# A two-layer hybrid decoder step on one core: ScalarE work behind VectorE issued later, branches in another order, pooling spread out, gates one pair ahead

## The chip, the core and the metric

The kernel runs on one core of one Trainium2 chip. The metric is device time in microseconds (us) of the whole launch, here the median of three runs. The engines named below are TensorE (PE in the profile), VectorE (DVE), ScalarE (ACT), GpSimd (POOL) and SyncE (SP, which here only issues transfers). Each works through its own instructions in order.

## The reference, cut to what matters

One step of two equal layers over 544 columns (512 prompt tokens and 8 x 4 new ones), all in f32 with a model width of 1024. A layer is a feed-forward block, a mixer, a second feed-forward block and a gated per-layer embedding. The change lies in the mixer alone:

```
h = rmsnorm(x, g_mix);  z = h @ w_in
u_a, v_a, b_gate, c_gate, x_b, x_c, gates = split(z)
v_a = layernorm(gelu(v_a));  y_a = (gelu(u_a) * (tril(w_s) @ v_a + b_s)) @ a_out      # branch a
y_b = (b_gate * short_conv(c_gate * x_b)) @ b_out                                      # branch b
y_c = ((window_mean(x_c, 2|4|8|16) - x_c) @ c_w * c_scale) @ c_out                     # branch c
g = sigmoid(gates)
x = x + (g0*y_a + g1*y_b + g2*y_c) @ w_o
```

The short convolution has three taps; the pooling has four channel groups with windows of 2, 4, 8 and 16 positions.

## The kernel before, in words

Activations lie transposed: 8 tiles of 128 channels x 544 columns. Every f32 product is made of three products of split operands, a high part rounded on ScalarE (L245 for weights, L362 for activations) and a low part, the difference, on VectorE (L250, L367). Weights come in units of 128 x 512 through the SP queue (L224, L227, L231), some with an accumulating transfer of the POOL queue on top (L232). `unit()` (L260) prepares them ahead of their use: the low part four units ahead, the high part five, the sum (L238) six, the load fifteen.

Two output tiles of `w_in` are made together by `pair()` (L736), which calls `s_pair()` (L568): a Strassen-Winograd scheme of seven half-size products, W21, R2, R3, W22, R1, W12, R4, each 12 matmuls (L326), 84 in all. Products that add into the same accumulator X need X copied by ScalarE first (L582 after W21, before R3; L584 after R3, before R1; L589 after R1, before R4). VectorE reads the others (L585, L587, L590, L592). The accumulators lie in four PSUM tiles of two halves each, taken in turn. Products of the branches' own output weights and of `w_o` go through `gemm()` (L306, matmuls of L303).

The order of the work is the order of the code. Each engine's queue is in that order, and what is to be issued later is put on two lists: `later` (a function and the number of ticks until it is issued) and `bg`, a queue of functions that `background()` spreads over a number of ticks. `tick()` (L175) runs once for each weight unit: once per product of `s_pair`, and once per `gemm` of four blocks. `flush()` issues at once all that is left.

The mixer runs: the first convolution pair by `gemm`; the v rows (L833, 120 matmuls of 512 columns into five PSUM halves; ScalarE takes the gelu of each, L807, VectorE its mean and variance, L808 and L809); three convolution pairs, each followed by `conv_in` (L746: product with the gate on VectorE, L751; two copies and the first tap on ScalarE, L756 to L765; two further taps on VectorE, L767); two pairs for `b_gate`; branch b; the pairs of x_c with the pooling steps (`pool_in` L898 to L910 on ScalarE, window sums L926, means L934, small fix-ups L939 and L940, then the split L362 and L367); a pair of u; branch c with `c_mix` (four small products by `c_w`, scaled by L961); the other pair of u; the four spatial products (`spatial`, L997); branch a; the product by `w_o`. In a branch, each step makes a pair of gates (sigmoid by L738 to L741) and then two `gemm`s, whose results are multiplied by the gates (L876) and added up (L881). `merge` (L856) splits the sum for `w_o`.

Of the kernel before, what the change touches and what calls it, by code (L numbers as in the profile page):

```python
# [17 lines left out]
KD = D // P  # L18
# [20 lines left out]
LOADS = 9  # L39
USE_MERGE = 51  # L40
AHEAD = 4
# [62 lines left out]
class Kern:  # L104
# [252 lines left out]

    def split_later(self, t_, aps, sls, n=1):
        nc = self.nc
        a, b = self.rpair()  # L360
        hi, lo, src = a[0][:, :], b[0][:, :], t_[0][:, :]
        nc.scalar.activation(hi, src, AF.Copy)  # L362
        aps.append((hi, lo))
        sls.extend((a, b))

        def fin():
            nc.vector.tensor_sub(lo, src, hi.bitcast(F32))  # L367
            self.drop(t_)

        if n:  # L370
            self.later.append((n, fin))
        return fin

# [350 lines left out]
    def mix(self, l, inp, nxt):  # L724
# [11 lines left out]
        def pair(z1, z2, f=None):  # L736
            s1, s2 = self.slot(), self.slot()
            self.s_pair("w_in", l, z1, z2, sets, s1, s2, (lambda out, ps: nc.scalar.activation(out, ps, f)) if f else None)  # L738
            if f:
                nc.scalar.activation(s2[0][:, :HT], s2[0][:, :HT], f)  # L740
                nc.scalar.activation(s1[0][:, :], s1[0][:, :], f)  # L741
            return s1, s2
# [3 lines left out]
        def conv_in(j, c_, x_, z_=None):  # L746
            c, x = c_[0], x_[0]
            sv = self.nt(self.cst[:, :], CB + TS)
            xp, xs_ = (z_[0][:, :SEQ], self.nt(z_[0][:, SEQ:T], TS)) if z_ else (x[:, CB:CCOLS], sv[:, :, CB:])
            nc.vector.memset(x[:, :CB], 0.0)  # L750
            nc.vector.tensor_mul(x[:, CB:CCOLS], xp, c[:, :SEQ])  # L751
            nc.vector.tensor_mul(sv[:, :, CB:], xs_, self.nt(c[:, SEQ:T], TS))
            if z_:
                self.drop(z_)
            o = j * NS * CB
            nc.scalar.activation(self.cso[:, SO_CP + j * CB:SO_CP + (j + 1) * CB], x[:, CCOLS - CB:CCOLS], AF.Copy)  # L756
            o = SO_CS + j * NS * CB
            nc.scalar.activation(self.nt(self.cso[:, o:o + NS * CB], CB), sv[:, :, TS:], AF.Copy)
            ys = self.nt(c[:, SEQ:T], TS)
            for k in range(3):  # L760
                o = PB_CW + (l * 3 + k) * G + j
                wk = self.par[:, o:o + 1]
                if k == 0:
                    nc.scalar.activation(c[:, :SEQ], x[:, 0:SEQ], AF.Copy, scale=wk)
                    nc.scalar.activation(ys, sv[:, :, 0:TS], AF.Copy, scale=wk)  # L765
                else:
                    nc.vector.scalar_tensor_tensor(c[:, :SEQ], x[:, k:k + SEQ], wk, c[:, :SEQ], op0=ALU.mult, op1=ALU.add)  # L767
                    nc.vector.scalar_tensor_tensor(ys, sv[:, :, k:k + TS], wk, ys, op0=ALU.mult, op1=ALU.add)
            self.drop(x_)
            conv[j] = c_  # L770

        def conv_state(j):
# [94 lines left out]

        def branch(br, ys, wn, mid=None):
            for m in range(0, KD, 2):
                ts = pair(Z_G + br * KD + m, Z_G + br * KD + m + 1, AF.Sigmoid)  # L870
                if m == 0 and mid:
                    mid()
                for i, t_ in enumerate(ts):
                    t = t_[0]
                    py, = self.gemm([(wn, l, m + i, ys, 0)])
                    nc.vector.tensor_mul(self.v2(t[:, :]), self.pv(py), self.v2(t[:, :]))  # L876
                    if len(macc) < KD:
                        macc.append(t_)
                        continue
                    mc = macc[m + i][0]  # L880
                    nc.vector.tensor_add(mc[:, :], mc[:, :], t[:, :])  # L881
                    self.drop(t_)
                    if br == 0 and self.used < USE_MERGE and len(merged) == m + i:
                        merge(m + i)
# [5 lines left out]
        self.background([v_stat] + [lambda i=i, f=f: f(i) for i in range(5) for f in (v_norm, v_bias)], 30)  # L890
        self.extra = EXTRA[4]
        branch(1, yb, "b_out", conv_done)
        self.drop(*yb_s)
        pooled, pooled_s = {}, {}
# [17 lines left out]
        def pool_steps(j, z_):  # L912
# [30 lines left out]

            return [begin] + [double] * (win.bit_length() - 1) + [mean, lambda: pool_out(j, st)]

# [29 lines left out]
        self.flush()  # L975
# [6 lines left out]
        u_in(0)  # L982

        def c_mid():
            self.flush()
            c_mix()

        branch(2, yc, "c_out", c_mid)
        self.drop(*yc_s)

        ya, ya_s = [], []

        def spatial(g):
# [13 lines left out]
            self.drop(us[g])  # L1007
            self.split_later(t_, ya, ya_s)
            if g == G - 1:
# [287 lines left out]
```

## Time and profile before

| | |
|---|---|
| median of 3 runs | 2452.64 us (2451.56 to 2452.81) |
| the profiled execution | 2452.78 us, its span 2451.1 us, granted clock 0.995 |
| busy, PE / DVE / ACT / POOL | 98% / 76% / 50% / 9% of the span |
| chain that ended last | PE 93%, DVE 3%, ACT 3%, issue 1% |
| mean DMA rate | 135 GB/s |

The page gives each engine's busy share; the chain that ended last follows the run back from its end and says at each step which engine held it up. The two mixers lie at about 389 to 799 us and 1598 to 2008 us of the span. A matmul that runs right behind another shows as one run with it; a gap in a timeline has in brackets how long the engine waited, and for whom.

### The profile page before, as it was taken

Reading aid. Unit: us, or ns where it says so; the run is one execution under the profiler, and the core shown is the slowest. Engines: PE = TensorE matmul, PEld = TensorE weight load, DVE = VectorE, ACT = ScalarE, POOL = GpSimd, SP = SyncE. Lnnn points to the kernel's source line nnn. Section 1 sums busy time; section 2 is a strip of 40 time slices with the busy share of each in tenths; the row PEclk is TensorE's granted clock in tenths of the full one; section 3 lists DMA queues with packets and bytes.
Section 4 is the critical chain, followed back from the end, with each engine's and each line's share of the span. In section 5 each row is a group of like instructions: output and inputs, shape, how many; then the busy total and the mean of one; then the engine's idle time right before and its main releaser. Section 6 shows DMA issues by size and latency. Waiting matters only on the chain.

```text
span 2451.1 us, 48091 instructions
## 1 busy us (share of the span) xinstructions
PE 2407.8 (98%) x18848; PEld 2386.7 (97%) x18848; DVE 1861.8 (76%) x3439; ACT 1215.0 (50%) x2357; POOL 226.3 (9%) x276
## 2 busy tenths in 40 slices
PE   8999999998999999999999999999989999999997
PEld 8999998998999999999999999989989999999997
DVE  7776777878678777768777776778787778777675
ACT  6444444646446544445554444546455554544452
POOL 1101000111110110100010110001101001101000
PEclk9999999999999999999999999999999999999999
DMA  6555561665554555555255554526545536556521
GB/s 204 141 146 143 147 168 27 175 146 130 151 148 121 134 143 144 154 133 161 59 144 136 144 156 127 162 60 159 149 126 146 151 95 154 153 125 158 139 84 37
DMA packets 180034, 329.78 MB, mean 135 GB/s; under 512 B 20256, under 2 KB 22560, under 8 KB 179808
## 3 DMA queue, kind: packets, MB, share of 16 engines
q1 hardware_dynamic: 141264, 255.92, 33.8%
q0 software_dynamic: 36672, 68.51, 16.7%
q8 instruction: 148, 2.42, 0.4%
q10 hardware_dynamic: 1872, 2.29, 0.3%
q14 instruction: 78, 0.64, 0.1%
HBM read 323.64 MB, written 2.99 MB: 133 GB/s over the span
## 4 chain that ended last, share of the span: by engine, by line
PE 93%; DVE 3%; ACT 3%; issue 1%; DMA 0%; DVEq 0%; ACTq 0%
PE ps L326 49%; PE ps L303 38%; PE ps L1094 2%; PE ps L833 2%; ACT s L245 1%; PE ps L531 0%; PE ps L517 0%; DVE s L926 0%; DVE s L250 0%; DVE s L1006 0%; ACT s L807 0%; ACT s L362 0%; DVE s L483 0%; ACT L738 0%; DVE s L238 0%
## 5 line engine op out<-in xcount | busy, mean ns | idle before, releaser
L326 PE MATMUL ps<-s,s 128*128 128x272 f32 x10332 | 1321.2, 289 | 18.2 <-ACT s L582 14.6
L326 PEld LDWEIGHTS ps<-s,s 128*128 128x128 f32 x10332 | 1307.7, 189 | 24.1 <-ACT s L582 18.4
L303 PE MATMUL ps<-s,s 128*128 128x272 f32 x7536 | 965.1, 288 | 8.2 <-ACT s L444 7.0
L303 PEld LDWEIGHTS ps<-s,s 128*128 128x128 f32 x7536 | 953.0, 189 | 9.8 <-ACT s L444 6.9
L250 DVE TENSOR_TENSOR s<-s,s 128x512 fp32r<-128x512 f32 x1211 | 812.5, 686 | 21.8 <-ACT s L245 19.9
L245 ACT ACTIVATE s<-s 128x512 fp32r<-128x512 f32 x1211 | 702.6, 623 | 230.8 <-DVE s L238 225.8
L232 POOL DMA_DIRECT2D s<-in_wts x246 | 210.7, 875 | 1941.4 <-DMA s<-in_wts 761.7
L582 ACT ACTIVATE s<-ps 128x272 f32<-128x272 f32 x123 | 48.7, 396 | 468.9 <-PE ps L326 468.9
L665 DVE SCALAR_TENSOR_TENSOR x<-ps,x 128x544 f32<-128x544 f32 x128 | 92.7, 724 | 184.1 <-PE ps L303 182.3
L238 DVE TENSOR_TENSOR s<-s,s 128x512 f32<-128x512 f32 x246 | 168.7, 686 | 0.0
L585 DVE TENSOR_TENSOR s<-ps,s 128x272 f32<-128x272 f32 x123 | 54.3, 442 | 113.8 <-ACT s L584 112.3
L584 ACT ACTIVATE s<-ps 128x272 f32<-128x272 f32 x123 | 48.8, 397 | 103.6 <-PE ps L326 102.2
L590 DVE TENSOR_TENSOR s<-ps,s 128x272 f32<-128x272 f32 x123 | 54.3, 442 | 56.6 <-ACT s L589 55.8
L589 ACT ACTIVATE s<-ps 128x272 f32<-128x272 f32 x123 | 48.7, 396 | 92.1 <-PE ps L326 92.0
L876 DVE TENSOR_TENSOR s<-ps,s 128x544 f32<-128x544 f32 x48 | 34.8, 725 | 68.2 <-PE ps L303 62.6
L616 ACT ACTIVATE s<-s 128x544 fp32r<-128x544 f32 x88 | 57.9, 658 | 37.1 <-DVE s L613 21.1
L619 DVE TENSOR_TENSOR s<-s,s 128x544 fp32r<-128x544 f32 x88 | 63.4, 721 | 6.1 <-ACT s L616 5.8
L610 ACT ACTIVATE s<-s 128x544 f32<-128x544 f32 x88 | 57.9, 658 | 19.6 <-DVE s L652 18.0
L626 DVE TENSOR_TENSOR s<-s,rstd 128x544 f32<-128x544 f32 x88 | 63.5, 722 | 0.1
L1094 PE MATMUL ps<-s,s 128*128 128x256 f32 (+1 forms) x480 | 61.6, 289 | 1.8 <-ACT rstd L533 1.8
L1094 PEld LDWEIGHTS ps<-s,s 128*128 128x128 f32 x480 | 60.5, 188 | 2.0 <-ACT rstd L533 2.0
L833 PE MATMUL ps<-s,s 128*128 128x512 f32 x240 | 56.9, 395 | 3.1 <-ACT s L807 3.1
(137 smaller groups left out, 1156.1 us busy)
## 6 DMA issues: line engine op xcount, KB each, us to landing
s<-in_wts SPq DMA_DIRECT2D x965, 256.0 KB, 3.3
s<-in_wts POOLq DMA_DIRECT2D x246, 256.0 KB, 5.1
x<-in_xT SPq DMA_DIRECT2D x4, 272.0 KB, 5.0
x<-in_xT ACTq DMA_DIRECT2D x4, 272.0 KB, 5.4
s<-in_pT POOLq DMA_DIRECT2D x4, 272.0 KB, 4.2
out_yT<-s SPq DMA_DIRECT2D x4, 144.0 KB, 1.8
out_yT<-s ACTq DMA_DIRECT2D x4, 144.0 KB, 1.8
s<-in_st_in POOLq DMA_DIRECT2D x2, 272.0 KB, 3.0
```

Of the source, the lines that this page charges most:

```text
L232: self.nc.gpsimd.dma_start(out=t, in_=src(1 if w == "R1" else 2, 4), accum_op=ALU.add)
L238: self.nc.vector.tensor_add(self.new_raw(w, u0, 2 if w == "R3" else 1), self.read_raw(a, u0), self.read_raw(b, u0))
L245: self.nc.scalar.activation(a[0][:, :UC], self.read_raw(w, u0), AF.Copy)
L250: self.nc.vector.tensor_sub(lo, self.read_raw(w, u0), hi.bitcast(F32))
L303: self.nc.tensor.matmul(ps[:, h, :HT], a, bh, start=first and i == 0, stop=last and i == 2)
L326: self.nc.tensor.matmul(ps, a, b, start=first and i == 0, stop=last and i == 2, skip_group_check=go_on)
L610: nc.scalar.activation(t[:, :], t[:, :], AF.Silu)
L619: nc.vector.tensor_sub(lo, o[:, :], hi.bitcast(F32))
L626: nc.vector.tensor_mul(o[:, :], o[:, :], self.rstd[:, :])
L665: nc.vector.scalar_tensor_tensor(xm, self.pv(pst[i]), 0.5, xm, op0=ALU.mult, op1=ALU.add)
L833: nc.tensor.matmul(vb[i], a[:, t0:t0 + P], b, start=(k == 0 and q == 0), stop=(k == KD - 1 and q == 2))
L1094: nc.tensor.matmul(ps, a, b[:, c], start=first and i == 0, stop=last and i == 2)
```

## The change

Line numbers of the rows `L...` of the changed kernel are up to 16 higher. The change does this:

- `split_later` can put both the high part (ScalarE) and the low part (VectorE) some ticks later; before, the high part was issued at once.
- In `pair` with a function (gelu, sigmoid), its application to the first output is issued one tick later.
- In `conv_in`, the first tap and the two copies on ScalarE come one tick after the product, the other taps two ticks after.
- The v rows are finished in the order 0, 2, 4, 1, 3, and their means and variances are put into the background of branch b.
- The branches run b, a, c instead of b, c, a. The pooling of windows 8 and 16 is spread over 18 ticks of branch a, that of windows 2 and 4 over 8 ticks at the end of branch a and the first gates of branch c. A step without work is put between the mean and the split.
- In branches a and c the gates are made one pair ahead of the `gemm`s that use them. The spatial products come two after each pair of u.
- `c_mix` goes through the windows from the longest to the shortest, its splits 1 to 5 ticks later.
- `USE_MERGE` is 57 instead of 51, and `merge` belongs to branch c.

```diff
-    def split_later(self, t_, aps, sls, n=1):
+    def split_later(self, t_, aps, sls, wait=0):
...
+        def first():
+            nc.scalar.activation(hi, src, AF.Copy)
...
+        if wait:
+            self.later.append((wait, first))
+        else:
+            first()
+        self.later.append((wait + 1, fin))
...
-                nc.scalar.activation(s1[0][:, :], s1[0][:, :], f)
+                self.later.append((1, lambda: nc.scalar.activation(s1[0][:, :], s1[0][:, :], f)))
...
+            product()
+            self.later += [(1, first_tap), (2, other_taps)]
...
-            self.split_later(b_, yb, yb_s)
+            self.split_later(b_, yb, yb_s, 1)
...
+
+        def v_sums(i):
             nc.vector.bn_stats(mv[:, i, 2:8], vt[i][:, :SEQ])
...
-        for i in range(5):
+        for i in (0, 2, 4, 1, 3):
             v_mm(KD - 1, w, i)
             v_in(i)
...
+        def gates(br, m):
+            return pair(Z_G + br * KD + m, Z_G + br * KD + m + 1, AF.Sigmoid)
...
-            return [begin] + [double] * (win.bit_length() - 1) + [mean, lambda: pool_out(j, st)]
+            return [begin] + [double] * (win.bit_length() - 1) + [mean, lambda: None, lambda: pool_out(j, st)]
...
         def c_mix():
-            fin = None
-            for j in range(G):
+            for i, j in enumerate(reversed(range(G))):
                 pc, = self.gemm([("c_w", l, 0, pooled[j], j)])
...
-                if fin:
-                    fin()
-                fin = self.split_later(t_, yc, yc_s, 0)
-            fin()
+                self.split_later(t_, yc, yc_s, 1 + i)
+            yc.reverse()
...
         self.flush()
-        self.background(pool_pair(2), 14)
-        fs = pool_pair(0)
-        self.flush()
-        self.background(fs, 12)
+        self.background([lambda i=i: v_sums(i) for i in range(5)] + [v_stat] + [lambda i=i, f=f: f(i) for i in range(5) for f in (v_norm, v_bias)], 30)
+        self.extra = EXTRA[4]
+        for m in range(0, KD, 2):
+            branch_out(1, m, gates(1, m), yb, "b_out")
...
-        branch(2, yc, "c_out", c_mid)
-        self.drop(*yc_s)
...
-        u_in(2)
-        for g in range(G):
+        for g in range(0, G, 2):
+            u_in(g)
+            self.flush()
             spatial(g)
-        branch(0, ya, "a_out")
+            spatial(g + 1)
+        ts = gates(0, 0)
+        for m in range(0, KD, 2):
+            nx = gates(0, m + 2) if m + 2 < KD else None
+            branch_out(0, m, ts, ya, "a_out")
+            ts = nx
+            if m == 0:
+                self.background(pool_pair(2), 18)
+            if m == 4:
+                self.background(pool_pair(0), 8)
         self.drop(*ya_s)
+        ts = gates(2, 0)
+        self.flush()
+        c_mix()
+        for m in range(0, KD, 2):
+            nx = gates(2, m + 2) if m + 2 < KD else None
+            branch_out(2, m, ts, yc, "c_out")
+            ts = nx
```

What stands on ScalarE at three places of layer 1, before and now. First the end of the v rows: the five gelus and the PSUM tile that each reads, and what follows them. Before:

```order
L807 ACTIVATE s_783_5079<-ps_73,cols 128x512
L807 ACTIVATE s_784_5080<-ps_73,cols 128x512
L807 ACTIVATE s_785_5081<-ps_72,cols 128x512
L807 ACTIVATE s_786_5082<-ps_72,cols 128x512
L807 ACTIVATE s_787_5083<-ps_74,cols 128x512
```

Now:

```order
L818 ACTIVATE s_783_5071<-ps_73,cols 128x512
L818 ACTIVATE s_785_5073<-ps_72,cols 128x512
L818 ACTIVATE s_787_5075<-ps_74,cols 128x512
L818 ACTIVATE s_784_5072<-ps_73,cols 128x512
L818 ACTIVATE s_786_5074<-ps_72,cols 128x512
```

Two gelus of the same PSUM tile no longer follow each other; two others lie between them.

Second, ScalarE from the end of the first convolution pair (the copy of its last product) into the next pair (the copy out of `ps_72` after its W21). Before, with the taps between the two:

```order
L597 ACTIVATE s_836_5326<-ps_71 128x272
L775 ACTIVATE cst<-s_777_4934 128x8x2
L756 ACTIVATE cso<-s_858_5464 128x2
L758 ACTIVATE cso<-cst 128x16
L764 ACTIVATE s_835_5325<-s_858_5464,par 128x512
L765 ACTIVATE s_835_5325<-cst,par 128x32
L245 ACTIVATE s_861_5479<-s_768_4864 128x512
L582 ACTIVATE s_860_5477<-ps_72 128x272
```

Now:

```order
L601 ACTIVATE s_836_5316<-ps_71 128x272
L786 ACTIVATE cst<-s_777_4934 128x8x2
L245 ACTIVATE s_861_5461<-s_768_4864 128x512
L586 ACTIVATE s_860_5459<-ps_72 128x272
L768 ACTIVATE s_835_5315<-s_858_5454,par 128x512
L769 ACTIVATE s_835_5315<-cst,par 128x32
L770 ACTIVATE cso<-s_858_5454 128x2
L772 ACTIVATE cso<-cst 128x16
```

The tap and the two copies moved behind the copy of the next pair's first product, which is L586 now.

Third, ScalarE in the pooling: before, at the end of the first window pair's steps (the split L362 of a mean, `pool_in` of the next window, another split, and then the copy of the first product of the u pair):

```order
L362 ACTIVATE s_1128_7205<-s_1108_7070 128x544
L903 ACTIVATE s_1130_7208<-s_1078_6907 128x512
L904 ACTIVATE s_1133_7211<-s_1078_6907 128x8x4
L907 ACTIVATE s_1133_7211<-s_777_4934 128x8x15
L908 ACTIVATE s_1077_6906<-s_1130_7208 128x15
L910 ACTIVATE s_1077_6906<-s_1133_7211 128x120
L362 ACTIVATE s_1134_7228<-s_1132_7210 128x544
L245 ACTIVATE s_1138_7236<-s_1095_6993 128x512
L582 ACTIVATE s_1137_7234<-ps_74 128x272
```

Now, in branch a, the split of the longest window (L366) and the pooling start of the next one (L910 on), at the end of the sigmoid of the third pair of gates and in the first product of the fourth:

```order
L742 ACTIVATE s_1214_7731<-ps_71 128x272
L744 ACTIVATE s_1214_7731<-s_1214_7731 128x272
L245 ACTIVATE s_1241_7894<-s_1207_7678 128x512
L745 ACTIVATE s_1213_7730<-s_1213_7730 128x544
L245 ACTIVATE s_1243_7925<-s_1204_7658 128x512
L366 ACTIVATE s_1246_7930<-s_1219_7752 128x544
L245 ACTIVATE s_1250_7962<-s_1212_7715 128x512
L586 ACTIVATE s_1249_7960<-ps_74 128x272
L910 ACTIVATE s_1253_7981<-s_1189_7590 128x512
```

The split stands a sigmoid and two weight splits after the pair's last copy, with two `gemm`s of PE ahead of the next copy; the next window's start comes after that copy and not before it.

## Rows read from the trace of the kernel before

**Rows 1.** Page, busy time of TensorE, share of the span, instructions:

```profile
PE 2407.8 (98%) x18848; PEld 2386.7 (97%) x18848; DVE 1861.8 (76%) x3439; ACT 1215.0 (50%) x2357; POOL 226.3 (9%) x276
```

**Rows 2.** Page, chain that ended last, share by engine:

```profile
PE 93%; DVE 3%; ACT 3%; issue 1%; DMA 0%; DVEq 0%; ACTq 0%
```

**Rows 3.** Chain in order of time, pieces of both mixers: start, us, what:

```profile
396.74 24.94 PE ps L833 x108
...
430.89 7.99 PE ps L326 x61
...
628.44 10.55 PE ps L326 x84
638.99 6.02 PE ps L303 x48
...
1606.71 25.07 PE ps L833 x108
...
1640.98 7.91 PE ps L326 x61
```

**Rows 4.** Timeline of PE, end of the v rows: start, us, instructions, [wait]:

```profile
422.45 1.66 PE L833 MATMUL ps<-s,s 128*128 128x512 f32 x6 [0.78 <-ACT s L807]
...
429.62 0.64 PE L326 MATMUL ps<-s,s 128*128 128x272 f32 x3 [0.56 <-DVE s L483]
```

**Rows 5.** Timeline of PE, convolution pairs:

```profile
453.48 11.23 PE L326 MATMUL ps<-s,s 128*128 128x272 f32 x84 [0.18 <-ACT s L582]
464.90 29.36 PE L326 MATMUL ps<-s,s 128*128 128x272 f32 x228 [0.18 <-ACT s L582]
```

**Rows 6.** Timeline of ACT behind a convolution pair:

```profile
440.06 0.20 ACT L756 ACTIVATE cso<-s 128x2 f32<-128x2 f32 x1 [0.65 <-DVE s L751]
```

**Rows 7.** Timeline of PE, pooling to the end of `c_mix`, both layers:

```profile
549.76 24.27 PE L326 MATMUL ps<-s,s 128*128 128x272 f32 x192
579.25 13.58 PE L326 MATMUL ps<-s,s 128*128 128x272 f32 x84 [5.22 <-ACT s L582]
...
601.00 4.80 PE L303 MATMUL ps<-s,s 128*128 128x272 f32 x34
...
611.70 10.73 PE L326 MATMUL ps<-s,s 128*128 128x272 f32 x84
...
1759.62 24.24 PE L326 MATMUL ps<-s,s 128*128 128x272 f32 x192
...
1820.84 10.69 PE L326 MATMUL ps<-s,s 128*128 128x272 f32 x84
```

**Rows 8.** Timeline of ACT in the pooling:

```profile
577.74 0.66 ACT L362 ACTIVATE s<-s 128x544 fp32r<-128x544 f32 x1 [3.02 <-DVE s L940]
...
578.82 0.38 ACT L582 ACTIVATE s<-ps 128x272 f32<-128x272 f32 x1
```

**Rows 9.** Stretches behind the pooling gap: busy (instructions) by engine, PEclk, DMA:

```profile
579.30:586.90 7.60, 7.60 (x38) 7.60 (x39) 6.55 (x14) 3.84 (x11) 1.63 (x2) 0.59 0.58 178
...
1789.10:1796.00 6.90, 6.90 (x38) 6.90 (x39) 6.50 (x14) 3.82 (x10) 0.86 (x1) 0.66 0.63 196
```

**Rows 10.** Timeline of PE, last spatial products and the pair behind them:

```profile
677.60 11.16 PE L326 MATMUL ps<-s,s 128*128 128x272 f32 x84
688.60 6.17 PE L303 MATMUL ps<-s,s 128*128 128x272 f32 x48
```

**Rows 11.** Groups by line, DVE: busy us, mean ns of one:

```profile
L250 DVE TENSOR_TENSOR s<-s,s 128x512 fp32r<-128x512 f32 x1211 | 812.5, 686 | 21.8 <-ACT s L245 19.9
...
L961 DVE TENSOR_SCALAR s<-ps,par 128x544 f32<-128x544 f32 x8 | 6.1, 779 | 0.0
```

**Rows 12.** Page, weight transfers by queue, us to landing:

```profile
s<-in_wts SPq DMA_DIRECT2D x965, 256.0 KB, 3.3
s<-in_wts POOLq DMA_DIRECT2D x246, 256.0 KB, 5.1
```

**Rows 13.** Timeline of POOL in the pooling:

```profile
584.90 0.86 POOL L232 DMA_DIRECT2D s<-in_wts  x1 [20.18 <-DVE s L250]
```

More of the change, by code (lines that the diff above doesn't have):

```diff
@@ L39 @@
 LOADS = 9
-USE_MERGE = 51
+USE_MERGE = 57
 AHEAD = 4
@@ L361, in split_later @@
         hi, lo, src = a[0][:, :], b[0][:, :], t_[0][:, :]
-        nc.scalar.activation(hi, src, AF.Copy)
         aps.append((hi, lo))
         sls.extend((a, b))
+        def first():
+            nc.scalar.activation(hi, src, AF.Copy)
         def fin():
@@ L368, in fin @@
             self.drop(t_)
-        if n:
-            self.later.append((n, fin))
-        return fin
+        if wait:
[3 more added lines that the diff above has]
+        self.later.append((wait + 1, fin))
     def gain(self, l, which, m):
@@ L749, in conv_in @@
             xp, xs_ = (z_[0][:, :SEQ], self.nt(z_[0][:, SEQ:T], TS)) if z_ else (x[:, CB:CCOLS], sv[:, :, CB:])
[L750 to L756, printed above, removed]
@@ L757, in conv_in @@
-            o = SO_CS + j * NS * CB
-            nc.scalar.activation(self.nt(self.cso[:, o:o + NS * CB], CB), sv[:, :, TS:], AF.Copy)
-            ys = self.nt(c[:, SEQ:T], TS)
[L760 to L768, printed above, removed]
@@ L769, in conv_in, with tap, product @@
-            self.drop(x_)
-            conv[j] = c_
+            ys = self.nt(c[:, SEQ:T], TS)
+            conv[j] = c_
+            def tap(k):
+                return self.par[:, PB_CW + (l * 3 + k) * G + j:PB_CW + (l * 3 + k) * G + j + 1]
+            def product():
+                nc.vector.memset(x[:, :CB], 0.0)
+                nc.vector.tensor_mul(x[:, CB:CCOLS], xp, c[:, :SEQ])
+                nc.vector.tensor_mul(sv[:, :, CB:], xs_, self.nt(c[:, SEQ:T], TS))
+                if z_:
+                    self.drop(z_)
@@ new lines, in first_tap, with other_taps @@
+            def first_tap():
+                nc.scalar.activation(c[:, :SEQ], x[:, 0:SEQ], AF.Copy, scale=tap(0))
+                nc.scalar.activation(ys, sv[:, :, 0:TS], AF.Copy, scale=tap(0))
+                nc.scalar.activation(self.cso[:, SO_CP + j * CB:SO_CP + (j + 1) * CB], x[:, CCOLS - CB:CCOLS], AF.Copy)
+                o = SO_CS + j * NS * CB
+                nc.scalar.activation(self.nt(self.cso[:, o:o + NS * CB], CB), sv[:, :, TS:], AF.Copy)
+            def other_taps():
+                for k in (1, 2):
+                    nc.vector.scalar_tensor_tensor(c[:, :SEQ], x[:, k:k + SEQ], tap(k), c[:, :SEQ], op0=ALU.mult, op1=ALU.add)
+                    nc.vector.scalar_tensor_tensor(ys, sv[:, :, k:k + TS], tap(k), ys, op0=ALU.mult, op1=ALU.add)
+                self.drop(x_)
@@ L866, in merge, with branch_out @@
             self.later += [(1, lambda: nc.scalar.activation(hi, src, AF.Copy)), (2, fin)]
[L868 to L884, printed above, removed]
+        def gates(br, m):
+            return pair(Z_G + br * KD + m, Z_G + br * KD + m + 1, AF.Sigmoid)
+        def branch_out(br, m, ts, ys, wn):
+            for i, t_ in enumerate(ts):
+                t = t_[0]
+                py, = self.gemm([(wn, l, m + i, ys, 0)])
+                nc.vector.tensor_mul(self.v2(t[:, :]), self.pv(py), self.v2(t[:, :]))
+                if len(macc) < KD:
+                    macc.append(t_)
+                    continue
+                mc = macc[m + i][0]
+                nc.vector.tensor_add(mc[:, :], mc[:, :], t[:, :])
+                self.drop(t_)
+                if br == 2 and self.used < USE_MERGE and len(merged) == m + i:
+                    merge(m + i)
         def conv_done():
             nc.gpsimd.dma_start(out=self.outs["co"][l], in_=self.cso[:, :])
-        self.flush()
[L890 to L893, printed above, removed]
         pooled, pooled_s = {}, {}
@@ L972, in mix @@
         self.flush()
-        self.background(pool_pair(2), 14)
-        fs = pool_pair(0)
-        self.flush()
-        self.background(fs, 12)
+        self.background([lambda i=i: v_sums(i) for i in range(5)] + [v_stat] + [lambda i=i, f=f: f(i) for i in range(5) for f in (v_norm, v_bias)], 30)
[3 more added lines that the diff above has]
+            if m == 0:
+                conv_done()
+        self.drop(*yb_s)
         us = []
@@ L980, in u_in @@
             us.extend(pair(Z_U + j, Z_U + j + 1, AF.Gelu_apprx_tanh))
[L982 to L986, printed above, removed]
-        branch(2, yc, "c_out", c_mid)
-        self.drop(*yc_s)
         ya, ya_s = [], []
@@ L1007, in spatial @@
             self.drop(us[g])
-            self.split_later(t_, ya, ya_s)
+            self.split_later(t_, ya, ya_s, 2 + g % 2)
             if g == G - 1:
@@ L1015, in mix @@
         rows[:] = [row("a_bs")]
-        u_in(2)
-        for g in range(G):
+        for g in range(0, G, 2):
+            u_in(g)
+            self.flush()
             spatial(g)
-        branch(0, ya, "a_out")
-        self.drop(*ya_s)
+            spatial(g + 1)
[4 more added lines that the diff above has]
+            ts = nx
+            if m == 0:
+                self.background(pool_pair(2), 18)
+            if m == 4:
+                self.background(pool_pair(0), 8)
+        self.drop(*ya_s)
+        ts = gates(2, 0)
[5 more added lines that the diff above has]
+            ts = nx
+        self.drop(*yc_s)
         self.drop(*sl)
```

## The prediction

> **What bounds the kernel now.** I read the busy times first [rows 1]: PE is busy for 98% of the span, so time can come only from PE's pauses and from stretches in which its matmuls run slow. The chain that ended last says the same [rows 2]: PE 93%, DVE and ACT 3% each. The second view is that chain in order of time [rows 3]. It gives PE's undisturbed pace: a pair of `s_pair` (84 matmuls of L326) takes 10.55 us, 48 matmuls of L303 take 6.02 us, so 0.1256 and 0.1254 us each. The third view is PE's timeline in the mixer, where four places run slower than that pace; the reader is to see there whom each first matmul behind a gap waited for, and in ACT's timeline that ACT was waiting itself, for VectorE, with PE's copy behind it.
>
> **The v rows.** The 108th matmul of L833 ends at 396.74 + 24.94 = 421.68, and with 61 matmuls of the first pair left PE goes on at 430.89 [rows 3]. In these 9.21 us it did 12 of L833 (12 x 0.231 = 2.77) and 23 of L326 (2.89): 3.55 us lost. In layer 2, by the same rows, 9.20 us for 2.79 + 2.89: 3.52. The rows of the gaps [rows 4] name two causes. PE waits for the gelu of row 0 before it may write row 1, which lies in the same PSUM tile, and likewise for row 3. Then it waits for L483, which stands on DVE behind five means and variances. The change takes both away. In the order 0, 2, 4, 1, 3 the gelu of a tile has the time of two rows (2 x 0.70 us for three matmuls each) where it needs 0.70. With the means gone, DVE's last two L483 follow ACT's last two splits: those end about 4.7 us after 421.68, the low parts at 5.45, and PE, which ends its rows at 2.78 and needs 1.51 us a product, wants the last low part at 5.67. So 0.2 us are to spare. Gain 3.55 + 3.52 = 7.1; if the margin fails, some 0.5 a layer come back.
>
> **The convolution pairs.** PE's pairs start at 453.48 and 464.90 [rows 5]: 11.42 us, 0.87 above the pace, three times a layer. PE waits for L582, the copy of W21, and ACT has L756 to L765 before it, of which L756 waits for VectorE's product L751 [rows 6]. In the new order these four stand behind the copy. That copy is due 1.5 us after the last pair ends and R3 needs it at 3.0; before it stand only the last copy, a small one and a weight split. The next copy of X is due at 4.5; ahead of it are now the tap, the copies and two splits, some 2.6 us begun at 1.9. So nothing is late. Gain 6 x 0.87 = 5.2. The first tap's VectorE part comes two ticks later, where DVE has slack.
>
> **The pooling.** From 549.76 to 611.70 [rows 7] PE does four pairs and 72 matmuls of L303: 42.20 + 9.03 = 51.23 us of work in 61.94, 10.7 lost; in layer 2, 1759.62 to 1820.84, 10.0. The largest piece is the 5.22 us gap, for L582. ACT's timeline shows why [rows 8]: a `flush` issues the rest of the window sums at once, ACT's L362 waits 3.02 us for L940, and PE's copy comes behind it, at 578.82. A second piece comes from the gap: behind it the granted clock is 0.59 and 0.66, between 1.2 and 2.4 GHz, for 38 matmuls in 7.60 and 6.90 us [rows 9], against 38 x 0.1256 = 4.77: 2.8 and 2.1 us. A third is `c_mix`: from 601.00, 10.7 us for 72 matmuls worth 9.03, 1.7 lost. In the new code no flush meets unfinished sums: the 15 steps of the long windows have 18 ticks, the 11 of the short ones 8, with 9 ticks of PE work before `c_mix`. The split of a mean stands a step later, and the start of a window behind the copy. All 20.7 go, the half clock with its cause.
>
> **The spatial products.** The pair behind four of them takes 688.60 - 677.60 = 11.0 us [rows 10], 0.45 too long, for splits on ACT in front of the copy. They are two and three ticks later now. Gain 0.9 in both layers.
>
> **What is new.** (1) Before `c_mix` DVE is nearly full. From the end of the last x_c pair PE has two `gemm`s, the first gates of branch c and four small products: 6.02 + 10.55 + 3.01 = 19.6 us until W21 of the next gates, which writes the PSUM tile of the first small product. VectorE must first have read that by L967 (L961 before). Ahead of it in its queue are, in that time, 10 weight operations, 2 gate products with their sums, 14 operations of pooling, small ones with them, 4 reads of products and 2 splits. At 0.60 us for a weight operation queued behind another (L250's 812.5 us over 1211 are 0.67 [rows 11]) I get 16.0 us, plus 2.8 in which it waits for PE and ACT; with one more L250 it reaches L967 at about 19.4 and is done 0.8 later: PE waits 0.65. With the full durations of the rows (0.686 and 0.779 [rows 11]) it is 3.1, and with a split less it is nothing. I take 0.65, since the queue is tight and back to back; 1.3 in both layers. (2) The start of the second window of a pair puts 1.2 us on ACT before a copy of X: 0.1 a layer. (3) Gates one pair ahead hold two more buffers, the pooling holds its own through branch a. Loads then come later, by how much the trace can't say; they are issued nine units (13.5 us) before their first use, and landing takes 3.3 + 5.1 with the accumulating transfer [rows 12], so 5.1 us are to spare: nothing taken, bound below. (4) One table load of ACT less in each layer, off the path; the two in branch b stand before copies with over 2 us of room.
>
> **Sum.** 7.1 + 5.2 + 20.7 + 0.9 = 33.9; less 1.3 and 0.2: 32.4 us. The profiled execution took 2452.78 (span 2451.1 and 1.7 around it), so 2420.4; the median of the runs is 0.14 lower: **2420.3 us**. All gone without a new wait would be 2418.7; all the new waits at their upper bounds (3.1 at `c_mix`, 0.5 at v, in each layer) 2426.
>
> **Rivals.**
> A. The pooling stall moves instead of going: DVE, filled by the sums in branch a, reads the accumulators late, and pairs wait one by one. For it: with every operation at its full duration a pair with its two `gemm`s and half a pooling pair costs DVE about 17.7 of PE's 16.6 us. Against it: back to back, operations overlap, and VectorE idles between pooling steps now. Price: half of the 20.7 stays, 2430.
> B. The ACT queue in the convolution and at v is late for another reason, another instruction that waits for VectorE having the copy behind it (the splits L245 also wait for L238). Against it: these waits are there now, in stretches that run at 10.55 a pair. Price: 12.3 stays, 2433.
> C. Slower: the weights come late. Loads wait for buffers that VectorE frees; the accumulating transfer at 584.90 had waited 20.18 us, for an L250 [rows 13]. If more held buffers and a fuller VectorE push the loads back by more than the 5.1 us to spare, each pair of branches a and c (10 a layer) waits for its two accumulated units. At one unit each, 1.5 us, that is 2 x 20 x 1.5 = 60 us against 33.9: 2479. It decides from 0.85 us a unit. Against it: half of that wait was PE's own gap, all the loads of the mixer stand in the same order on SP, and ACT shows no wait for a weight transfer in the mixer now.
>
> For C there is a rule: the Trainium skill (SBUF — State Buffer, "SBUF: two separate sides") says that VectorE operations of some kinds lock GpSimd out of a shared port, so that transfers issued by GpSimd start late. The issue at 584.90 took 0.86 us while VectorE was full around it [rows 13], so here the trace does not show it. As an estimate from the page's figures (620 ns alone, 3100 beside a VectorE operation) a late issue would take 2.5 of the 5.1 us and change nothing; only one that repeats through a stretch gives C's time, and by the row the forecast's stays.
>
> **How the numbers follow.** Forecast 0.72; A 0.15; B 0.08; C 0.05. The likeliest gives 2417 to 2427 by its bounds; with A and B the range goes to 2432, which leaves C and the worst of B outside. This kernel's measurement can tell 0.2%, 4.9 us, from no change. Forecast, A and B are all faster by more than that; C splits into slower and a part where it eats the gain. Faster 0.94, same 0.02, slower 0.04.
>
> **What would show it.** In the new profile: the 24 matmuls of the first pair after the v rows start without a gap, the convolution pairs at 10.55 us; no PE gap over 1 us in branches a and c, and PEclk at 1.00 through both mixers; at the second gates of branch c a gap of some 0.65 us for L967. PE's busy time should fall too, by the slow stretches. Wrong would be a PE gap for L245 or L250 in branch a (A or C), a clock below 0.9 in a mixer, or pairs over 10.8 us.

## The result, and the profile after

The changed kernel takes 2421.33 us (median of four executions) where the kernel before takes 2452.43: ratio 0.9871, 95% interval 0.9852 to 0.9891. Three of the four took 2419.65 to 2421.51 us; the fourth took 6041.94 at an undiminished granted clock, no trace shows why, and the ratio leaves it out. In a second comparison it took 2421.86 (2420.25 to 2421.93) against 2451.99, ratio 0.9876 (0.9861 to 0.9891). The profiled execution has a span of 2419.8 us against 2451.1: 31.3 us less.

The page of the changed kernel, busy time of TensorE and the shares of the chain that ended last, beside [rows 1, 2]:

```profile
PE 2395.4 (99%) x18848; PEld 2381.8 (98%) x18848; DVE 1856.7 (77%) x3439; ACT 1208.4 (50%) x2355; POOL 225.6 (9%) x276
PE 97%; DVE 2%; ACT 1%; issue 0%; DMA 0%; DVEq 0%; ACTq 0%
```

What PE waited for in the changed kernel, by waiting line and releaser; the columns are us in total, times, longest. The first row is the start of the kernel; L521, L535 and L1110 stand in the last block, and all four have their match before:

```profile
PE ps L303 <- ACT s L448: 7.3, 1, 7.3
PE ps L521 <- DVE acc L1142: 3.0, 1, 3.0
PE ps L326 <- ACT s L586: 1.9, 3, 0.7
PE ps L535 <- DVE s L528: 1.8, 1, 1.8
PE ps L1110 <- ACT rstd L537: 1.8, 1, 1.8
PE ps L326 <- DVE s L967: 1.4, 2, 0.7
```

The same view of the kernel before, three of its rows, the largest of those that the change went for (L582 is now L586, L807 L818, L483 L487):

```profile
PE ps L326 <- ACT s L582: 14.6, 13, 5.2
...
PE ps L833 <- ACT s L807: 3.1, 4, 0.8
...
PE ps L326 <- DVE s L483: 2.4, 4, 0.6
```

These and two small ones (L367 1.2, L584 0.3) are 21.6 us of idle time before; of them and the new L967, 3.3 are left. The three left for L586 stand in feed-forward blocks (experiment 10). Idle time thus fell by 18.3 and the span by 31.3, so a wait costs more than its idle time, the half clock behind some of them included (below).

PE's timeline in layer 1 of the changed kernel (start, us, instructions, in brackets the wait ahead of the first of them):

```profile
396.43 27.88 PE L846 MATMUL ps<-s,s 128*128 128x512 f32 x120
424.14 63.47 PE L326 MATMUL ps<-s,s 128*128 128x272 f32 x504
487.45 6.19 PE L303 MATMUL ps<-s,s 128*128 128x272 f32 x48
...
657.33 10.67 PE L326 MATMUL ps<-s,s 128*128 128x272 f32 x84
667.84 3.17 PE L303 MATMUL ps<-s,s 128*128 128x272 f32 x24
671.70 10.79 PE L326 MATMUL ps<-s,s 128*128 128x272 f32 x84 [0.70 <-DVE s L967]
```

Where [rows 4, 5] have gaps and pairs of 11.42 us, all 120 v rows now stand in one row and the 504 matmuls of the pairs behind them in another: 487.45 - 424.14 = 63.31 us, 0.1256 each, which is the undisturbed pace. Where [rows 7] have the gap of 5.22 us and a slow `c_mix`, there is one gap of 0.70, for L967, and 0.68 in layer 2. The granted clock, which was 0.59 and 0.66 in [rows 9], is 1.00 through the branches (stretch, its us, busy us by engine, then PEclk, DMA share, GB/s):

```profile
487.40:721.50 234.10, 233.40 (x1855) 232.54 (x1853) 187.60 (x351) 127.43 (x262) 26.36 (x32) 1.00 0.58 148
```

To compare kernels whose branches have another order I cut PE's timeline at the same matmul, counted in the trace. Stage V runs from the first v row to the first product of branch b (624 matmuls), stage B from there to the first matmul of `w_o` (1984), stage E from the first matmul of the last block to its last one (all in us, from one profile each; the rows are named after the experiments below):

| kernel | V, layers 1 and 2 | B, layers 1 and 2 | E |
|---|---|---|---|
| before | 97.51, 97.38 | 260.66, 260.01 | 72.96 |
| changed | 91.02, 90.97 | 250.59, 250.29 | 74.45 |
| v rows alone | 93.74, 93.66 | 260.34, 259.80 | 73.01 |
| taps alone | 94.76, 94.68 | 260.56, 259.64 | 74.10 |
| v order back | 93.13, 93.07 | 250.59, 250.29 | 72.86 |
| v sums back | 92.96, 92.87 | 250.52, 250.36 | 74.49 |
| pooling flushed | 91.04, 91.14 | 255.44, 256.57 | 74.35 |
| gates of a not ahead | 91.03, 91.09 | 249.68, 249.46 | 72.88 |
| gates of c not ahead | 91.03, 91.20 | 254.58, 254.61 | 72.82 |

Changed against before: V 12.90 us less, B 19.79 less, E 1.49 more, and 0.1 in the rest.

### The profile page after: what moved, and what is told of

Its sections match the earlier page's. It is cut to its first block, busy times and chain, and to the rows that moved or that the text cites. A ratio compares the mean times of both kernels' runs of the same rounds, so it can differ in the third digit from the quotient of the medians.

```text
span 2419.8 us, 48050 instructions
## 1 busy us (share of the span) xinstructions
PE 2395.4 (99%) x18848; PEld 2381.8 (98%) x18848; DVE 1856.7 (77%) x3439; ACT 1208.4 (50%) x2355; POOL 225.6 (9%) x276
## 4 chain that ended last, share of the span: by engine, by line
PE 97%; DVE 2%; ACT 1%; issue 0%; DMA 0%; DVEq 0%; ACTq 0%
PE ps L326 52%; PE ps L303 39%; PE ps L1110 2%; PE ps L846 2%; PE ps L535 0%; PE ps L521 0%; PE ps L995 0%; DVE s L250 0%; ACT L614 0%; DMA par<-in_par 0%; DVE s L1155 0%; DVE s L630 0%; DVE s L646 0%; PE ps L997 0%; DVE s L369 0%
## 5 line engine op out<-in xcount | busy, mean ns | idle before, releaser
L250 DVE TENSOR_TENSOR s<-s,s 128x512 fp32r<-128x512 f32 x1211 | 812.0, 685 | 20.1 <-ACT s L245 19.0
L245 ACT ACTIVATE s<-s 128x512 fp32r<-128x512 f32 x1211 | 705.2, 622 | 224.7 <-DVE s L238 222.2
L586 ACT ACTIVATE s<-ps 128x272 f32<-128x272 f32 x123 | 48.8, 397 | 461.7 <-PE ps L326 455.9
L238 DVE TENSOR_TENSOR s<-s,s 128x512 f32<-128x512 f32 x246 | 168.6, 685 | 0.0
L620 ACT ACTIVATE s<-s 128x544 fp32r<-128x544 f32 x88 | 57.8, 657 | 37.2 <-DVE s L617 21.2
L1110 PE MATMUL ps<-s,s 128*128 128x256 f32 (+1 forms) x480 | 63.2, 294 | 1.8 <-ACT rstd L537 1.8
L1110 PEld LDWEIGHTS ps<-s,s 128*128 128x128 f32 x480 | 62.0, 193 | 2.0 <-ACT rstd L537 2.0
L617 DVE TENSOR_TENSOR s<-s,s 128x544 f32<-128x544 f32 x82 | 58.9, 719 | 0.4
```

The lines of the kernel that those rows point to most:

```text
L238: self.nc.vector.tensor_add(self.new_raw(w, u0, 2 if w == "R3" else 1), self.read_raw(a, u0), self.read_raw(b, u0))
L245: self.nc.scalar.activation(a[0][:, :UC], self.read_raw(w, u0), AF.Copy)
L250: self.nc.vector.tensor_sub(lo, self.read_raw(w, u0), hi.bitcast(F32))
L617: nc.vector.tensor_mul(o[:, :], o[:, :], t[:, :])
L1110: nc.tensor.matmul(ps, a, b[:, c], start=first and i == 0, stop=last and i == 2)
```

## Experiments

Each was measured beside the kernel before on the same chip; the times are medians of four executions or more unless said otherwise.

**1. The v rows alone, in the kernel before.**

```
         def v_in(i):
             nc.scalar.activation(vt[i][:, :SEQ], vb[i], AF.Gelu_apprx_tanh, ...)
+
+        def v_sums(i):
             nc.vector.bn_stats(mv[:, i, 2:8], vt[i][:, :SEQ])
             nc.vector.bn_aggr(mv[:, i, 0:2], mv[:, i, 2:8])
...
-        for i in range(5):
+        for i in (0, 2, 4, 1, 3):
             v_mm(KD - 1, w, i)
             v_in(i)
...
-        self.background([v_stat] + [...], 30)
+        self.background([lambda i=i: v_sums(i) for i in range(5)] + [v_stat] + [...], 30)
```

> The kernel before with the v rows changed alone (order 0, 2, 4, 1, 3; means and variances moved behind the rows). Theory (the v rows, the convolution, the pooling and the spatial products are four separate stalls, each of them ACT or DVE waiting in order with PE's copy behind it): 7.1 us less, 2445.3; PE has no gap between L833's last rows and the first products in either layer, and the other gaps of the kernel before stand as they were (5.2 us behind L582 in the pooling among them). Rival (the stalls hang together: time won early is given back at the next one, since VectorE or the loads set the pace): under 3 us less, over 2449.

2444.89 us, ratio 0.9970 (0.9959 to 0.9981), 7.2 less than before. Stage V fell by 3.77 and 3.72. In PE's list of waits those for L807 and L483 are gone, and that for the copies stands as it was:

```profile
PE ps L326 <- ACT s L582: 14.6, 13, 5.3
```

**2. The taps of the convolution alone, in the kernel before.**

```
-            nc.scalar.activation(self.cso[:, ...], x[:, CCOLS - CB:CCOLS], AF.Copy)
-            ...
-            nc.scalar.activation(c[:, :SEQ], x[:, 0:SEQ], AF.Copy, scale=wk)
-            ...
+            product()
+            self.later += [(1, first_tap), (2, other_taps)]
```

> The kernel before with the taps of the convolution alone issued one and two products later. Theory: the six convolution pairs go from 11.42 to 10.55 us, 5.2 us less, 2447.2; nothing else moves. Rival (another ACT instruction that waits for VectorE stands before the copy then, as rival B has it): pairs stay over 11 us, under 2 us less.

2448.43 us, ratio 0.9983 (0.9974 to 0.9992), 3.6 less. By that number alone the theory would be 1.6 short. The stages tell more: V fell by 2.75 and 2.70, 5.45 in all, as expected, and the pairs run at the full pace, without a gap:

```profile
430.97 49.21 PE L326 MATMUL ps<-s,s 128*128 128x272 f32 x390 [0.63 <-DVE s L483]
```

Most of what is missing is in stage E, 1.14 longer in this profile, which has nothing of the change in it (experiment 8). The gains of experiments 1 and 2 add up to 12.94 in stage V, and the whole change has 12.90 there: the stalls are separate ones.

**3 and 4. One half of the v change undone, in the changed kernel:** the order 0 to 4 again; and `v_sums(i)` again directly behind `v_in(i)`.

```
-        for i in (0, 2, 4, 1, 3):
+        for i in range(5):
```

```
-        def v_sums(i):
             nc.vector.bn_stats(mv[:, i, 2:8], vt[i][:, :SEQ])
...
-        self.background([lambda i=i: v_sums(i) for i in range(5)] + [v_stat] + [...], 30)
+        self.background([v_stat] + [...], 30)
```

> The changed kernel with the v rows in the order 0 to 4 again; the means stay moved. Theory (two causes that add up: the PSUM tile shared by two rows, and the means in front of L487): the waits for the gelu come back, 4 of 0.78 us, so 3.1 us more, 2424.4, and no wait for L487. Rival (the means were the one cause and the waits for the gelu only hid behind it): under 1 us more.

> The changed kernel with the means and variances again directly behind each gelu; the order 0, 2, 4, 1, 3 stays. Theory: five of 0.87 us behind the first gelu end at about 426.6 in layer 1, four L487 of 0.63 us follow; PE waits 1.3 us for the second and 0.85 for the fourth, 2.15 a layer, 4.3 us more, 2425.6. Rival (the order alone sets the v rows, the means have time enough): under 1 us more.

2424.63 us (ratio 0.9888, 0.9875 to 0.9902) and 2424.55 (0.9887, 0.9873 to 0.9900), 3.3 and 3.2 more than the changed kernel. Stage V grew by 2.11 and 2.10 with the old order, by 1.94 and 1.90 with the old place of the sums. Both causes are real and neither covers the other. The old order, PE's timeline:

```profile
422.16 1.66 PE L846 MATMUL ps<-s,s 128*128 128x512 f32 x6 [0.78 <-ACT s L818]
424.60 1.66 PE L846 MATMUL ps<-s,s 128*128 128x512 f32 x6 [0.78 <-ACT s L818]
426.10 6.17 PE L326 MATMUL ps<-s,s 128*128 128x272 f32 x47
```

and the sums back in their place:

```profile
424.71 2.69 PE L326 MATMUL ps<-s,s 128*128 128x272 f32 x20
428.23 0.64 PE L326 MATMUL ps<-s,s 128*128 128x272 f32 x3 [0.84 <-DVE s L487]
429.50 10.68 PE L326 MATMUL ps<-s,s 128*128 128x272 f32 x83 [0.63 <-DVE s L487]
```

The second came 0.5 us under its 4.3. My expectation for the first was 1.1 us low over both layers (3.1 against 4.21), and the rows say why. I had counted idle time alone, 2 x 0.78 a layer. The six matmuls between two gaps take 1.66 us to the end of the last, where six in a stream take 6 x 0.231 = 1.39: 0.27 more per gap, 0.54 a layer, which is the difference. Behind 24 matmuls of 272 columns it is 0.16 (3.17 us against 24 x 0.1256 = 3.01). A gap is priced by the length of its stage, not by its bracket.

**5. The pooling flushed before the first gates of branch c**, not after them.

```
+        self.flush()
         ts = gates(2, 0)
-        self.flush()
         c_mix()
```

> The changed kernel with one flush moved: what is left of the short windows is issued at once before the first gates of branch c, not after them. Theory (a flush that meets unfinished sums puts the splits L366, which wait for VectorE, in front of the copy L586): two L366 wait for the means, the copy comes at about 665.5 in layer 1, PE has a gap of 5.3 us there in each layer, and behind it the granted clock falls to half for some 38 matmuls (2.1 to 2.8 us) as it did behind the gap of 5.22; the wait for L967 (0.7) goes. Sum 14 us more, 2435 (2430 if the clock stays). Rival (the order of the branches and the gates one pair ahead removed the stall, not the spreading): under 2 us more.

2432.22 us, ratio 0.9920 (0.9905 to 0.9934), 10.9 more than the changed kernel where I expected 14. Stage B grew by 4.85 and 6.28. The old picture of [rows 7, 8] is back, in ACT's queue:

```profile
664.08 0.66 ACT L366 ACTIVATE s<-s 128x544 fp32r<-128x544 f32 x1 [1.40 <-DVE s L947]
664.64 0.61 ACT L245 ACTIVATE s<-s 128x512 fp32r<-128x512 f32 x1
665.16 0.38 ACT L586 ACTIVATE s<-ps 128x272 f32<-128x272 f32 x1
```

in PE's timeline:

```profile
658.14 3.17 PE L326 MATMUL ps<-s,s 128*128 128x272 f32 x24
665.59 9.09 PE L326 MATMUL ps<-s,s 128*128 128x272 f32 x60 [4.28 <-ACT s L586]
674.52 3.18 PE L303 MATMUL ps<-s,s 128*128 128x272 f32 x24
```

and in the granted clock behind the gap (columns as above):

```profile
665.50:669.00 3.50, 3.41 (x16) 3.41 (x17) 2.49 (x4) 1.49 (x5) 0.00 (x0) 0.57 0.68 210
669.00:674.50 5.50, 5.50 (x46) 5.50 (x45) 5.01 (x10) 2.57 (x6) 1.69 (x2) 1.00 0.87 205
```

The gap is 4.28 us where I expected 5.3, the slow stretch 3.5 us at 0.57 in layer 1; in layer 2, behind the same gap of 4.28, the clock is 0.50 for 5.0 us from 1865.0, and that layer lost more. The wait for L967 is gone, as expected, since the sums are over by then. So a flush with unfinished sums makes the stall in the new order of the branches too, with the half clock behind it. It brings back 11.13 of the 19.79 us that stage B had gained. Whether the spreading alone would have been enough in the old order no run shows.

**6 and 7. The gates no longer one pair ahead**, in branch a alone; and in branch c alone, there with the small products in their old order and a flush behind them.

```
-        ts = gates(0, 0)
         for m in range(0, KD, 2):
-            nx = gates(0, m + 2) if m + 2 < KD else None
-            branch_out(0, m, ts, ya, "a_out")
-            ts = nx
+            branch_out(0, m, gates(0, m), ya, "a_out")
```

```
-            for i, j in enumerate(reversed(range(G))):
+            for i, j in enumerate(range(G)):
...
-                self.split_later(t_, yc, yc_s, 1 + i)
-            yc.reverse()
+                self.split_later(t_, yc, yc_s)
+            self.flush()
...
-            nx = gates(2, m + 2) if m + 2 < KD else None
-            branch_out(2, m, ts, yc, "c_out")
-            ts = nx
+            branch_out(2, m, ts if m == 0 else gates(2, m), yc, "c_out")
```

> The changed kernel with the gates of branch a no longer one pair ahead; those of branch c stay ahead. Theory: nothing in branch a needs them ahead; the short windows now run beside the last gates of branch a and end before the first gates of branch c, so that VectorE reaches L967 earlier and the wait of 0.7 us goes in both layers: 0 to 1.4 us less, 2420 to 2421. Rival (the gates ahead are what keeps PE from waiting): gaps for L893 or L888 in branch a, over 3 us more.

> The changed kernel with the gates of branch c no longer one pair ahead, the small products in their old order with a flush behind them. Theory: the gates ahead are worth something at one place only, behind the small products: PE waits there some 2.0 us a layer for the split of the first and the following results instead of 0.7 for L967, so 2.6 us more (1 to 4), 2424. Rival (each pair of branch c needs the gates ahead): gaps at each of the four pairs, over 8 us more.

Branch a: 2418.01 us, ratio 0.9861 (0.9844 to 0.9877), 3.3 less than the changed kernel where I expected 0 to 1.4. Of that, 1.74 are in stage B (0.91 and 0.83: about the idle time of 0.70 and 0.68, and 0.16 for each gap) and 1.57 in stage E, which has nothing of the edit in it. PE waits for nothing in branch a, and the wait for L967 is gone: VectorE stands idle before it, waiting for PE.

```profile
668.48 3.03 DVE L967 TENSOR_SCALAR s<-ps,par 128x544 f32<-128x544 f32 x4 [0.61 <-PE ps L303]
```

Branch c: 2428.34 us, ratio 0.9901 (0.9886 to 0.9915), 7.0 more where I expected 2.6 (1 to 4). Stage B grew by 3.99 and 4.32. The place is the one I named, behind the small products, and no other pair waits:

```profile
668.54 0.77 PE L303 MATMUL ps<-s,s 128*128 128x272 f32 x4 [0.28 <-ACT s L366]
670.64 4.81 PE L303 MATMUL ps<-s,s 128*128 128x272 f32 x24 [1.33 <-DVE s L369]
676.47 5.80 PE L303 MATMUL ps<-s,s 128*128 128x272 f32 x44 [1.01 <-DVE s L369]
```

Two things make up the rest: the three waits are 2.62 us and not 2.0, and the clock is at half speed from 670.6 to 674.0, so that 24 matmuls take 4.81 us and not 3.01:

```profile
670.60:674.00 3.40, 3.36 (x15) 3.36 (x16) 2.16 (x3) 1.07 (x3) 0.00 (x0) 0.51 0.90 205
```

So in branch a the gates ahead buy nothing and cost 0.9 a layer. At `c_mix` they are worth some 4 us a layer together with the new order of the small products and the later splits; the run undoes all three, and what each is worth alone it does not show.

**8. The changed kernel once more**, for the 1.5 us of stage E.

> The changed kernel once more. Its first profile has 3.41 us of half clock near the end of the kernel (from 2387 us), which the kernel before and the one with the gates of branch a not ahead do not have; the last stage took 74.45 us against 72.9. Theory (this piece comes and goes from run to run and is no part of the change): the median stays between 2419.6 and 2421.6, and the runs spread over some 1.5 us or the new profile has no such piece. Rival (it belongs to the change): the piece is there again and no run lies under 2420.5.

2421.86 us; three executions at 2421.81 to 2421.93 with a mean granted clock of 0.997 and one at 2420.25 with 0.998. The new profile has the slow piece too (E 74.16). So neither text is right as it stands. The piece is in both profiles; by the times and the mean clocks it is in most executions and not in each, though no profile shows one of this kernel without it. In the same wait for L537 the changed kernel and the one of experiment 6 part:

```profile
2386.39 18.48 PE L1110 MATMUL ps<-s,s 128*128 128x288 f32 x126 [1.76 <-ACT rstd L537]
```

```profile
2384.24 17.00 PE L1107 MATMUL ps<-s,s 128*128 128x288 f32 x126 [1.76 <-ACT rstd L537]
```

The first row is of the changed kernel, the second of the kernel with the gates of branch a not ahead. The same 126 matmuls behind the same wait take 1.48 us longer. The code there is the same; why the clock falls in one and not in the other stays open.

**9. L967 on ACT, and L620 delayed by a product**, in the changed kernel.

```
-                nc.vector.tensor_scalar_mul(self.v2(t_[0][:, :]), self.pv(pc), self.par[:, o:o + 1])
+                nc.scalar.activation(self.v2(t_[0][:, :]), self.pv(pc), AF.Copy, scale=self.par[:, o:o + 1])
...
-                fin = (e0, dz, e1, dr, d2, d3)
+                fin = (e0, dz, e1, dr, None, d2, d3)
```

> The changed kernel with two further edits: L967 goes from VectorE to ACT, and the split L620 of the last plain group of each feed-forward block is issued one product later, behind the first copy L586. Theory (the same ACT blocking is left at three places, 0.65, 0.63 and 0.63 us, and VectorE's backlog costs 0.70 and 0.68): all five gaps go, 3.3 us less, 2418.0. Rival (the gaps move to the next instruction): within 1 us of 2421.3.

2421.27 us, ratio 0.9873 (0.9858 to 0.9888): no gain, the rival is right. PE waits for L967 as long as before, 0.66 us, now on ACT:

```profile
670.43 0.65 ACT L745 ACTIVATE s<-s 128x544 f32<-128x544 f32 x1
670.98 0.62 ACT L245 ACTIVATE s<-s 128x512 fp32r<-128x512 f32 x1
671.50 2.51 ACT L967 ACTIVATE s<-ps,par 128x544 f32<-128x544 f32 x4
```

ACT reaches it no earlier than VectorE did: the copies and sigmoids of the gates stand before it, themselves late by ACT's waits for L238 (1.38) and L947 (0.71). The other edit did not move L620 past the copy: a `flush` in `ffn`, between the plain group and the first pair, issues whatever is pending.

**10. The split really behind the copy, with the gates of branch a not ahead.** What is pending of the plain group is put back behind that flush.

```
+                if first and not start:
+                    fin = (e0, dz, e1, dr)
+                    self.late = [(1, d2), (2, d3)]
...
                 if j == plain:
                     self.flush()
+                    self.later += self.late
+                    self.late = []
```

> The changed kernel with the gates of branch a not ahead (as before, 2418.0) and, in the three feed-forward blocks that begin behind another block, the split L620 of the first plain group issued one product later, behind the copy L586 and not ahead of it in a flush. Theory: the last three gaps for L586 (0.65, 0.63, 0.63 us) and some 0.2 to 0.3 us of slower first matmuls behind each go: 1.9 to 2.7 us less, 2415.3 to 2416.1. Rival (the gap goes to the next reader, as it did when L967 went to ACT): 2418.

2415.50 us (2414.50 to 2416.71), ratio 0.9852 (0.9837 to 0.9867): faster than both kernels, 6.4 us less than the changed one in the same comparison. Its line numbers are one higher here: L587 is the copy, L621 the split. ACT's timeline at the start of a feed-forward block:

```profile
791.65 0.40 ACT L587 ACTIVATE s<-ps 128x272 f32<-128x272 f32 x1 [0.44 <-PE ps L327]
792.77 0.66 ACT L621 ACTIVATE s<-s 128x544 fp32r<-128x544 f32 x1 [0.72 <-DVE s L631]
```

and PE's, which in the changed kernel has a gap of 0.65 us behind the first 24 of these matmuls:

```profile
789.95 10.22 PE L327 MATMUL ps<-s,s 128*128 128x272 f32 x80
```

The stretch between the first `w_o` and the second layer's v rows, which holds two of the three places, is 1.70 us shorter than in experiment 6, the one behind the second mixer, with the third, 0.76: 2.46 in all, 0.82 a place.

**11 and 12. A shorter lead of the weight loads** (`LOADS = 9` to 6, and to 4, the latter in a single execution), for the case in which the weights come late.

> The changed kernel with its weight loads issued six units ahead instead of nine. The lead is then 6 x 1.51 = 9.0 us, and an accumulated unit lands 3.3 + 5.1 = 8.4 us after its first issue. Theory (5.1 us of the lead were to spare): the same, within 2 us of 2421. Rival (the lead has no slack, because late buffers eat it): PE waits for L245 or L250 at many pairs, over 10 us more.

> The changed kernel with its weight loads issued four units ahead. The lead is 6.0 us, 2.4 less than the 8.4 of an accumulated unit. Theory (the lead decides, as the case in which the weights come late was priced): a pair, which has two accumulated units beside each other, waits up to 2.4 us; 123 pairs, up to 295 us more, and at least 60. Rival (the waiting of a transfer is hidden by the four units between its use and its split): under 20 us more.

Six units: 2427.67 us, ratio 0.9905 (0.9889 to 0.9922), 5.8 more than the changed kernel, where the theory said within 2. Four units: 2435.9. With six, stage B is the same (250.48 and 250.42) and no pair waits for a weight. The cost is behind `w_o`, where PE waits for the sums of squares, once in each layer; behind the second of these waits 42 matmuls take 7.04 us, behind the first 5.53:

```profile
PE ps L521 <- DVE acc L389: 3.1, 2, 1.6
```

VectorE has one more unit of weights to split there, L250 with a wait for ACT and L238; in the changed kernel L487 follows the first of these rows at once:

```profile
765.25 0.69 DVE L250 TENSOR_TENSOR s<-s,s 128x512 fp32r<-128x512 f32 x1 [0.76 <-ACT s L245]
766.96 0.69 DVE L250 TENSOR_TENSOR s<-s,s 128x512 fp32r<-128x512 f32 x1 [1.02 <-ACT s L245]
767.57 0.69 DVE L238 TENSOR_TENSOR s<-s,s 128x512 f32<-128x512 f32 x1
768.17 1.42 DVE L487 TENSOR_TENSOR s<-s,s 128x272 fp32r<-128x272 f32 x3
```

`LOADS` also enters the rule by which weights are split early (`fits`), which I had not counted. With four, stage B is 1.35 and 2.36 us longer, and the stretches behind the two `w_o` are 4.2 and 5.5 longer. That is 14.0 in all, in one execution, not the 60 and more of the text, although the lead is then shorter than the landing. Weights do come late there, but seldom: L238 waits seven times for a weight transfer, 11.0 us in all, and L245 three times, 3.8 us. Why the other units are not late the rival's reason would explain (a unit's split stands four more units ahead of its use, and these take up the lateness); no run shows it apart from the earlier splits.

## Why the prediction was right

Forecast 2420.3, measured 2421.33, inside the range and inside the forecast's own 2417 to 2427. The steps:

- **The v rows.** 7.1 predicted, 7.49 in experiment 1 alone. Both named causes hold (experiments 3 and 4). The margin of 0.2 us for L487 held: the pair behind the rows starts without a gap.
- **The convolution pairs.** 5.2 predicted, 5.45 in experiment 2, at 10.55 us a pair. Rival B, another instruction ahead of the copy, is not there.
- **The pooling and the spatial products.** Less the new waits, stage B was to gain 10.7 + 0.45 - 0.75 = 10.40 in layer 1 and 10.0 + 0.45 - 0.75 = 9.70 in layer 2; it gained 10.07 and 9.72. Experiment 5 shows a flush with unfinished sums as a cause of such a gap, with the half clock as its second piece. The third piece, `c_mix`, was not undone by itself. Rival A is not there: PE waits for no VectorE result in branch a.
- **The wait for L967.** 0.65 predicted, 0.70 and 0.68 measured; without it stage B is 0.91 and 0.83 shorter. VectorE reached L967 19.6 us after the x_c pair, 19.4 in my working; but it had 12 weight operations to do where I had 11, and waited 2.0 us where I had 2.8. The two errors partly cancel, so that close a hit, between bounds of nothing and 3.1, is in part luck. My working was of VectorE's queue alone. Experiment 9 shows ACT's as late at that moment, and experiment 6 what fills both: the sums of the short windows, which run on into the first gates of branch c.
- **The gates ahead at no cost.** True of the buffers: in the mixers neither L245 nor L238 waits for a weight transfer. But in branch a they push the short windows against `c_mix`, and that is the wait for L967; I had put the two side by side and not seen that one makes the other.
- **Rival C.** Its condition is not met, as no split waits for a weight, and its price was far too high: 60 us, where experiment 12 lost 14.0 with a lead shorter than the landing. The issue on GpSimd takes 877 ns beside a VectorE that is busy for 77% of the span, against 875 before (line, us busy and mean ns in the changed kernel):

```profile
L232 POOL DMA_DIRECT2D s<-in_wts x246 | 210.8, 877 | 1948.4 <-DMA s<-in_wts 717.0 <-ACT s L245 287.3 <-PE ps L326 193.7
```

The rule weighed there, by which VectorE locks GpSimd out of a shared port (the Trainium skill, SBUF — State Buffer, "SBUF: two separate sides"), is not shown by this trace either.

- **What the sum left out.** The stages that I priced gained 32.7 us against 32.4. The last block lost 1.49, by a half clock behind a wait that was there before; no step looked at that block, and the forecast is 1.0 low against the median by it. `USE_MERGE` and the moved `merge` were neither priced nor run by themselves.

## What to carry to other kernels

Where a copy that TensorE waits for shares an in-order engine with work that needs another engine's fresh result, look for that result behind every `flush` and every "issue now": each such place is a stall of its own, and the gains add up. Price a stall by the length of its stage against the same matmuls at the undisturbed pace, since idle time alone missed 0.27 us for each gap behind matmuls of 512 columns, 0.16 behind those of 272, and the half clock. Issue ahead only what hides a wait: the gates one pair ahead, with the small products in the order that goes with them, were worth 4 us a layer behind `c_mix`, and they cost 0.9 in branch a, where they only crowded what follows.

## What the runs showed of the hardware that I had not expected

The granted clock fell to half behind idle times much shorter than the 5.22 us of [rows 7]: behind 0.28 and 1.33 us in experiment 7 (0.51 from 670.6 to 674.0), and behind 1.76 us in the last block (0.60 from 2386.3 to 2390.0), where it fell in the profiles of some kernels and not of others with the same code there, and cost 1.48 us. In the v rows before, four waits of 0.56 to 0.78 us within 10 us left it at 1.00 (columns as above):

```profile
421.70:431.00 9.30, 6.58 (x36) 5.26 (x37) 7.05 (x16) 5.46 (x9) 0.00 (x0) 1.00 0.00 0
```

What decides between these is open.
